# A streaming encoder layer: the indexer's query tiles computed with one moving product of 448 columns for the high and low part of x

## The chip, the cores and the metric

The kernel runs on one core of a Trainium2 chip. The metric is the time of one execution on the device in microseconds (us), the median of several. One further execution is recorded by the profiler, and its trace is what the prediction reads. The engines are called PE (TensorE, matrix products; PEld are its weight loads), ACT (ScalarE), DVE (VectorE), POOL (GpSimd) and SP (SyncE, which here only issues DMAs). PE writes its results to PSUM, eight banks of 512 fp32 columns; ACT and DVE copy them to SBUF.

## The reference

One step of a layer with two branches, for 256 new frames and 32 sampled frames (T = 288 together). Everything starts from one projection of x (288 x 1024) with w_in, whose columns are cut into queries, keys, values and gates of both branches. What matters here is the sparse-attention branch's indexer: eight small query heads qi of 64 each (512 columns of the projection), one indexer key per frame ki and a weight per head wi. They score every key, and each query keeps the best quarter.

```python
p = x @ w_in
(qa, ka, va, oa, za, ia, fa, qb, kb, vb, zb, qi, ki, wi, ga, gb) = jnp.split(p, cuts, axis=-1)
...
sc = jnp.einsum('bqhd,bsd->bqhs', qi, ki).astype(jnp.float32) * (IDX_DIM ** -0.5)
score = jnp.einsum('bqh,bqhs->bqs', wi.astype(jnp.float32) * (IDX_HEADS ** -0.5), jax.nn.relu(sc))
...
_, idx = lax.top_k(score, k_sel)
```

The first 64 frames see only 64 keys and keep all of them, so their indexer queries aren't needed: of qi only the frames 64 to 287 are computed, 224 columns.

## The kernel before

All operands are fp32. To compute an accurate product on PE at the rate of a reduced type, the kernel splits each operand into a high part (a cast to fp32r, by ACT) and a low part (the difference, by DVE), and sums three products: high times high, low x times high weight, high x times low weight.

The work is a list of tiles (`ORDER`), each 128 columns of a weight matrix. Position 0 is the small tile "sm" (indexer key, gates, head weights: 80 columns), positions 1 to 4 are the four indexer query tiles ("qi", two heads each), then qb 0, kb 0, qb 1, kb 1, qb 2 at positions 5 to 9, and so on to the output projection "wo". Weights lie in partitions by k (eight slices of 128), x is transposed: moving operands are `xh[:, k]` and `xl[:, k]`, 288 frames.

The first five tiles (`FIRST = 5`) are computed together while their data arrive: `lead[k]` holds slice k of x and of the five tiles' weights. For k = 0 raw fp32 is used in one product; for k = 1 to 7 `first_products` (L1019 to L1030) runs three groups of five products: high weights with xh, high weights with xl, low weights with xh. Before the data are there, PE runs 15 products of constants (`keep_warm`, L163 to L167). Each of the five tiles has a bank of its own from the ring "side".

From position 5 on the main loop (L1156 to L1170) takes one tile per step t: it issues the loads, splits the weights of later tiles (`split_hi`, L143: ACT casts a whole tile to wh; `split_lo`, L151: DVE makes wl), copies finished tiles out of PSUM (`evac`, L888), and issues the 24 products of tile t (`product`, L974), in the middle of which `side()` issues what is due at this step: scores, gates, attention. Results from tile 5 on go into a ring of two banks ("proj", `out_bank`, L1014), so the products of tile t need the result of tile t - 2 to be copied out.

The order in each engine's queue is the order in which the program emits: the whole body is under a manual schedule. The first five tiles are copied out over the first steps (`held`, L1155): tiles 0 and 1 at step 5, tile 2 at step 6, tile 3 at step 7, tile 4 at step 8. Per step the emitted order is, for t below 8 (`CALM`): `evac(t - 1)`, the held tiles, `split_hi(t + 3)`, `split_lo(t + 2)`; from 8 on: the held tile, `split_lo(t + 2)`, `evac(t - 1)`, `split_hi(t + 3)`. At step 6 `side()` also issues `small_parts` (L275): ACT's copy of the indexer key, DVE's copy into the other half of the partitions, ACT's cast to `kih`, DVE's `kil`, ACT's gate row.

A query tile is copied out by `evac_qi` (L412): ACT casts five pieces from PSUM into the high halves of `qst` and `qis`, then DVE subtracts, writing the low parts into the other half of the partitions, so that one later product covers high and low part of a head.

Late in the program `load_affine` (L1042) reuses the room of xl for z and of xh for the LayerNorm constants.

Of the kernel before, what the change touches and what calls it, by code (L numbers as in the profile page):

```python
# [11 lines left out]
F32R = mybir.dt.float32r  # L12
BF = mybir.dt.bfloat16
AF = mybir.ActivationFunctionType
OP = mybir.AluOpType
# [4 lines left out]
D = 1024  # L20
TP = 256
TS = 32
T = TP + TS
KT = D // 128
# [1 line left out]
BH, BD = 8, 128  # L26
IH, ID = 8, 64
CHUNK = 64
WARM = 15
MID = 4  # L30
FIRST = 5
LATE = 5
# [1 line left out]
SMALL = 80  # L34
LEAD = T + SMALL + 128 * (FIRST - 1)
CALM = 8
PAST = 256
ALPHA = 2.0 ** 0.25
LN_EPS = 1e-5
# [19 lines left out]
def tile_order():  # L59
    order = [("sm", 0)] + [("qi", j) for j in range(4)]  # L60
    for h in range(BH):
        order += [("qb", h), ("kb", h)]
        if h == 3:
            order += [("vb", j) for j in range(8)]
    for h in range(AH):
        for n in ("qa", "ka"):
            order += [(n, 2 * h), (n, 2 * h + 1)]
    order += [("va", j) for j in range(8)]
    order += [("zb", j) for j in range(8)]
    for h in range(AH):  # L70
        for j in (2 * h, 2 * h + 1):
            order += [("oa", j), ("za", j)]
    for j in range(8):
        order += [("gb", j), ("wb", j)]
    for j in range(8):
        order += [("ga", j), ("wa", j)]
    order += [("wo", k) for k in range(KT)]
    return order


ORDER = tile_order()
# [4 lines left out]
def ap_of(t, offset, dims):  # L86
    return bass.AP(tensor=t.tensor, offset=t.offset + offset, ap=dims)
# [3 lines left out]
def body(ctx, tc, a, o):  # L91
    nc = tc.nc
    pe, act, dve, pool, sp = nc.tensor, nc.scalar, nc.vector, nc.gpsimd, nc.sync
# [5 lines left out]
    def sb(name, shape, dt=F32, tag=None, bufs=1):  # L99
        return P.tile(shape, dt, name=name, tag=tag or name, bufs=bufs)  # L100

    def bank(name, n=512):
        return ps.tile([128, 512], F32, name=name, tag="side", bufs=6)
# [19 lines left out]
    store, lazy, masked = {}, {}, []  # L123
# [5 lines left out]
    def load_tile(t):  # L129
        if t >= NT or t in loaded:  # L130
            return
        loaded.add(t)
        stage[t] = sb(f"wst{t}", [128, KT * 128], tag="wst", bufs=8)
        sp.dma_start(stage[t], a["w"][:, t - FIRST])

    def pair(name):
        if name == NT - 1:
            own = sb("wown", [128, 2, KT * 128], F32R, tag="a1")
            return own[:, 0], own[:, 1]
        return (sb(f"wh{name}", [128, KT * 128], F32R, tag="wh", bufs=4),  # L140
                sb(f"wl{name}", [128, KT * 128], F32R, tag="wl", bufs=4))

    def split_hi(t):  # L143
        if t >= NT or t in high:
            return
        load_tile(t)
        split[t] = pair(t)
        act.copy(split[t][0], stage[t])  # L148
        high.add(t)

    def split_lo(t):  # L151
        if t >= NT:
            return
        wh, wl = split[t]
        dve.tensor_tensor(wl, stage[t], wh.bitcast(F32), OP.subtract)  # L155


    xh = sb("xh", [128, KT, T], F32R)
    xl = sb("xl", [128, KT, T], F32R)
    wp = bank("warm_p")  # L160
    ones = nc.const_aps.tensor(1.0, (128, 256), BF)

    def keep_warm(n):  # L163
        for _ in range(n):
            pe.matmul(wp[:, :256], lhsT=ones[:, :128], rhs=ones, start=True, stop=True)  # L165

    keep_warm(WARM)  # L167

    early = sb("early", [128, 2064], tag="v1l")
    bms = early[:, 512:1088].rearrange("p (g t) -> p g t", g=2)  # L170
# [16 lines left out]
    for k in range(KT):  # L187
        raw = lead[k]
# [9 lines left out]
        wh, wl = pair(f"_k{k}")  # L198
# [15 lines left out]
    load_tile(FIRST + 4)  # L214
    sp.dma_start(cki, ap_of(a["cache_idx_k"], 0, [[0, 2], [PAST, 64], [1, PAST]]))

# [74 lines left out]
    def sample_keys():  # L291
        for c, keys in ((slice(0, PAST), cki), (slice(PAST, T), kiT[:, TP:T])):
            act.copy(ksh[:, c], keys)
            dve.tensor_tensor(ksl[:, c], keys, ksh[:, c].bitcast(F32), OP.subtract)
# [113 lines left out]
    kil = sb("kil", [128, TP], F32R, tag="hn", bufs=2)  # L408
    ksh = sb("ksh", [128, PAST + TS], F32R, tag="qph")
    ksl = sb("ksl", [128, PAST + TS], F32R, tag="qpl")  # L410

    def evac_qi(j, p):  # L412
        half = (slice(0, 64), slice(64, 128))
        parts = [(e, slice(t0, t1), slice(c, c + t1 - t0))
                 for e, t0, t1, c in ((0, 64, 128, 128), (0, 128, 256, 0), (1, 64, 256, 192))]
        for e, new, c in parts:
            act.copy(qst[half[e], j, c], p[half[e], new])
        for e in range(2):
            act.copy(qis[half[e], e, j], p[half[e], TP:T])
        for e, new, c in parts:  # L420
            own, other = half[e], half[1 - e]
            dve.tensor_tensor(qst[other, j, c], p[own, new], qst[own, j, c].bitcast(F32), OP.subtract)
        for e in range(2):
            own, other = half[e], half[1 - e]
            dve.tensor_tensor(qis[other, e, j], p[own, TP:T], qis[own, e, j].bitcast(F32), OP.subtract)
# [79 lines left out]
    def load_cache_k():  # L505
        lazy["ckT"] = sb("ckT", [128, 8, PAST], tag="a4")
        sp.dma_start(lazy["ckT"], a["cache_k"])
# [380 lines left out]
    def evac(t, p):  # L888
# [4 lines left out]
        if n == "sm":  # L893
            evac_small(p)
        elif n == "qi":
            evac_qi(j, p)
        elif n == "qb":
            act.copy(qbT[:, j], q)
# [75 lines left out]
    def product(t, side):  # L974
        n, j = ORDER[t]
        if n == "wo":
            natural(t, 0)
            side()
            natural(t, 1)
            return None  # L980
        h, l = moving(n)
        wh, wl = split.pop(t)
        p = out_bank(t)
        for k in range(KT):
            if k == MID:
                side()
            c = slice(128 * k, 128 * k + 128)
            pe.matmul(p[:, :T], lhsT=wh[:, c], rhs=h[:, k], start=(k == 0), stop=False)  # L988
            pe.matmul(p[:, :T], lhsT=wh[:, c], rhs=l[:, k], start=False, stop=False)  # L989
            pe.matmul(p[:, :T], lhsT=wl[:, c], rhs=h[:, k], start=False, stop=(k == KT - 1))  # L990
        return p
# [22 lines left out]
    def out_bank(t):  # L1014
        if t < FIRST:
            return bank(f"pj{t}")
        return ps.tile([128, 512], F32, name=f"pj{t}", tag="proj", bufs=2)

    def first_products():  # L1019
        p = [out_bank(t) for t in range(FIRST)]  # L1020
        for k, (wh, wl) in enumerate(leads):
            raw = lead[0][:, 0:T]
            for w, x in ((wh, raw),) if k == 0 else ((wh, xh[:, k]), (wh, xl[:, k]), ([wl], xh[:, k])):
                for t in range(FIRST):
                    new = slice(CHUNK if ORDER[t][0] == "qi" else 0, T)
                    part = w[0] if t < 2 else w[-1]
                    c0, c1 = (max(0, SMALL + 128 * i) for i in (t - 1, t))
                    pe.matmul(p[t][:c1 - c0, new], lhsT=part[:, c0:c1], rhs=x[:, new],  # L1028
                              start=(k == 0), stop=(k == KT - 1 and w[0] is wl))
        return p  # L1030


# [7 lines left out]
        sp.dma_start(lazy["xs"], ap_of(a["x_nat"], TP * D, [[256, 4], [D, TS], [1, 256]]))  # L1040

    def load_affine():  # L1042
        lazy["z"] = sb("z_", [128, 2, D], tag="xl")
        gb = sb("lngb", [128, 2, D], tag="xh")
        lazy["g"], lazy["b"] = gb[:, 0], gb[:, 1]
        sp.dma_start(gb, ap_of(a["ln_gb"], 0, [[0, 128], [D, 2], [1, D]]))
        for i, n in enumerate("gb"):
            sp.dma_start(lazy[n + "s"], ap_of(a["ln_gb"], D * i, [[256, 4], [0, TS], [1, 256]]))

    at(POS["ga", 3], load_tail)  # L1050
    at(POS["wo", 0], load_affine)

    def statistics(b, r, records):
# [89 lines left out]
    def side():  # L1143
        for fn, args in jobs.pop(cur[0], []):
            fn(*args)
        for g in list(procs):
            if next(g, StopIteration) is StopIteration:
                procs.remove(g)

    first = first_products()  # L1150
    for t in (FIRST, FIRST + 1):
        split_hi(t)
# [3 lines left out]
    for t in range(FIRST, NT - LATE):  # L1156
        cur[0] = t
        for i in range(FIRST, t + 10):
            load_tile(i)
        if FIRST < t < CALM:  # L1160
            evac(t - 1, prev)
        for i in held.get(t, ()):
            evac(i, first[i])
        if t < CALM:
            split_hi(t + 3)
        split_lo(t + 2)
        if t >= CALM:
            evac(t - 1, prev)
            split_hi(t + 3)
        prev = product(t, side)  # L1170
# [84 lines left out]
```

## Time and profile before

| what | us |
|---|---|
| median of 3 runs | 413.38 (413.21 to 413.8) |
| the profiled execution | 413.82 |
| its span, first to last instruction | 412.1 |
| PE busy | 407.7 |
| DVE busy | 316.6 |
| ACT busy | 215.2 |
| POOL busy | 193.0 |

The span leaves out what lies before the first and behind the last instruction. Busy PE time is modelled at its ends, since products are pipelined: how fast they run is read from the distance between their starts. In the rows of the trace the first number is the start in us from the span's start, the second the duration; then come engine, line, operation, tiles written and read, shape and count. A bracket says how long the engine was idle before, and what ended that; where an instruction waited for several things, the one named is the one that came last by the record.

Page of the profile, the costliest groups:

```profile
L989 PE MATMUL pj<-xl,wh 128*128 128x288 f32 x704 | 207.7, 295 | 0.0
L988 PE MATMUL pj<-xh,wh 128*128 128x288 f32 x704 | 207.6, 295 | 0.0
L990 PE MATMUL pj<-xh,wl 128*128 128x288 f32 x704 | 207.5, 295 | 0.0
L155 DVE TENSOR_TENSOR wl<-wst,wh 128x1024 fp32r<-128x1024 f32 x111 | 138.2, 1246 | 22.8 <-ACT wh L148 22.6
L148 ACT CAST wh<-wst 128x1024 fp32r<-128x1024 f32 x111 | 116.3, 1048 | 16.3 <-PE pj L989 5.1
```

Behind the bar stand the busy us, the mean ns of one instruction, and the engine's idle time before the group.

### The profile page before, as it was taken

What the parts mean: (1) busy time and instruction counts of PE and PEld (TensorE: products, weight loads), DVE (VectorE), ACT (ScalarE), POOL (GpSimd) and SP (SyncE); (2) the same over time, 40 slices, a digit from 0 to 9 for tenths busy, and PEclk for the clock granted to TensorE, in tenths of its full rate; (3) what the DMA queues carried; (4) which work ended last, traced back from release to release, by engine and by line L of the source; (5) the groups of instructions that cost most, each with busy time, mean ns of one, the idle gap of its engine ahead of it and who ended that gap; (6) DMA issues with size and microseconds to landing.
All of it is one profiled execution on the core that took longest, in us unless ns stands there. A gap on an engine that the chain in (4) does not pass through costs nothing.

```text
span 412.1 us, 8540 instructions
## 1 busy us (share of the span) xinstructions
PE 407.7 (99%) x3148; PEld 398.0 (97%) x3148; DVE 316.6 (77%) x653; ACT 215.2 (52%) x418; POOL 193.0 (47%) x448
## 2 busy tenths in 40 slices
PE   9999999999999999999999999999999999999996
PEld 7999999999999999999989999999999999999686
DVE  4679879998895878887969877988675566676574
ACT  4787463443765665576645545655434334555202
POOL 0200059993388657769800028547899744000021
PEclk9999999999999999999999999999999999999999
DMA  8987979787955655559944674455656557554014
GB/s 290 389 303 207 310 233 300 271 206 240 386 161 154 226 160 158 166 188 201 286 131 118 167 251 115 144 153 146 171 155 195 163 159 254 175 157 156 2 44 179
DMA packets 43151, 81.09 MB, mean 197 GB/s; under 512 B 20682, under 2 KB 25542, under 8 KB 42182
## 3 DMA queue, kind: packets, MB, share of 16 engines
q1 hardware_dynamic: 42390, 79.73, 62.8%
q10 hardware_dynamic: 720, 0.82, 0.6%
q8 instruction: 24, 0.39, 0.4%
q14 instruction: 17, 0.14, 0.1%
HBM read 73.38 MB, written 9.06 MB: 200 GB/s over the span
## 4 chain that ended last, share of the span: by engine, by line
PE 99%; ACT 0%; ACTq 0%; issue 0%
PE pj L989 27%; PE pj L990 27%; PE pj L988 27%; PE yn L1007 5%; PE pj L1028 4%; PE yn L1011 1%; PE warm_p L165 1%; PE ix L437 0%; PE al L593 0%; PE s L657 0%; PE av L626 0%; PE c L741 0%; PE c L739 0%; PE os L569 0%; PE c L740 0%; PE n L676 0%
## 5 line engine op out<-in xcount | busy, mean ns | idle before, releaser
L989 PE MATMUL pj<-xl,wh 128*128 128x288 f32 x704 | 207.7, 295 | 0.0
L988 PE MATMUL pj<-xh,wh 128*128 128x288 f32 x704 | 207.6, 295 | 0.0
L990 PE MATMUL pj<-xh,wl 128*128 128x288 f32 x704 | 207.5, 295 | 0.0
L155 DVE TENSOR_TENSOR wl<-wst,wh 128x1024 fp32r<-128x1024 f32 x111 | 138.2, 1246 | 22.8 <-ACT wh L148 22.6
L988 PEld LDWEIGHTS pj<-xh,wh 128*128 128x128 f32 x704 | 132.4, 188 | 0.6 <-issue 0.5
L989 PEld LDWEIGHTS pj<-xl,wh 128*128 128x128 f32 x704 | 132.4, 188 | 0.0
L990 PEld LDWEIGHTS pj<-xh,wl 128*128 128x128 f32 x704 | 132.3, 188 | 0.0
L148 ACT CAST wh<-wst 128x1024 fp32r<-128x1024 f32 x111 | 116.3, 1048 | 16.3 <-PE pj L989 5.1
L120 POOL COPY pt<-bm 32x96 f32<-32x96 f32 x128 | 48.8, 381 | 19.9 <-DVE bm L609 10.7
L120 POOL COPY kaT<-kn 32x128 f32<-32x128 f32 x64 | 30.1, 470 | 5.1 <-DVE kn L707 2.5
L120 POOL COPY vn<-qaT 32x128 f32<-32x128 f32 x64 | 29.0, 454 | 2.6
L120 POOL COPY hn<-qaT 32x128 f32<-32x128 f32 x32 | 15.6, 487 | 12.1 <-DVE qaT L683 5.7
L120 POOL COPY hn<-ht 32x128 f32<-32x128 f32 x32 | 14.6, 458 | 9.3 <-DVE ht L683 8.0
L965 POOL COPY mxs<-sg 128x32 f32<-128x32 f32 x8 | 1.7, 211 | 37.0 <-DVE sg L964 36.9
L988 PE MATMUL pj<-bah,wh 128*128 128x288 f32 x64 | 18.9, 296 | 0.0
L989 PE MATMUL pj<-bal,wh 128*128 128x288 f32 x64 | 18.9, 296 | 0.0
L990 PE MATMUL pj<-bah,wl 128*128 128x288 f32 x64 | 18.9, 296 | 0.0
L988 PE MATMUL pj<-bbh,wh 128*128 128x288 f32 x64 | 18.9, 295 | 0.0
L989 PE MATMUL pj<-bbl,wh 128*128 128x288 f32 x64 | 18.9, 295 | 0.0
L990 PE MATMUL pj<-bbh,wl 128*128 128x288 f32 x64 | 18.8, 294 | 0.0
L951 ACT ACTIVATE sg<-pj 128x288 f32<-128x288 f32 x16 | 6.6, 411 | 23.0 <-PE pj L990 23.0
L885 ACT CAST mxh<-sg 128x288 fp32r<-128x288 f32 x8 | 3.5, 433 | 22.1 <-DVE sg L964 22.1
(470 smaller groups left out, 654.1 us busy)
## 6 DMA issues: line engine op xcount, KB each, us to landing
wst<-in_w SPq DMA_DIRECT2D x112, 512.0 KB, 4.4
wst_k<-in_first SPq DMA_DIRECT2D x6, 440.0 KB, 7.9
rscr<-rrow SPq DMA_DIRECT2D x2, 768.0 KB
out_k<-kbT SPq DMA_DIRECT2D x1, 1152.0 KB, 10.2
vrows<-vat SPq DMA_DIRECT2D x8, 144.0 KB, 1.8
stC<-in_state_C SPq DMA_DIRECT2D x1, 1028.0 KB
out_C_sample<-stC SPq DMA_DIRECT2D x1, 1028.0 KB
bm<-rscr SPq DMA_DIRECT2D x1, 1024.0 KB
```

Of the source, the lines that this page charges most:

```text
L120: pool.tensor_copy(out(quads[k], quads[i]), turned(quads[i], quads[k]))
L148: act.copy(split[t][0], stage[t])
L155: dve.tensor_tensor(wl, stage[t], wh.bitcast(F32), OP.subtract)
L165: pe.matmul(wp[:, :256], lhsT=ones[:, :128], rhs=ones, start=True, stop=True)
L885: act.copy(lazy[hi][:, j], v)
L951: act.activation(sg, q, AF.Sigmoid)
L988: pe.matmul(p[:, :T], lhsT=wh[:, c], rhs=h[:, k], start=(k == 0), stop=False)
L989: pe.matmul(p[:, :T], lhsT=wh[:, c], rhs=l[:, k], start=False, stop=False)
L990: pe.matmul(p[:, :T], lhsT=wl[:, c], rhs=h[:, k], start=False, stop=(k == KT - 1))
L1007: pe.matmul(p, lhsT=x[:, k, r], rhs=w[:, c], start=first and i == 0, stop=last and i == 2)
L1011: pe.matmul(p[32 * q:32 * q + 32, 0:256], lhsT=lazy["mxs"][:, k], rhs=stage[t][:, 256 * q:256 * q + 256], start=first, stop=last)
L1028: pe.matmul(p[t][:c1 - c0, new], lhsT=part[:, c0:c1], rhs=x[:, new], start=(k == 0), stop=(k == KT - 1 and w[0] is wl))
```

## The change

For the query tiles and k = 1 to 7, the two products that share the high weights (with xh and with xl, 224 columns each) become one product of 448 columns: xh and xl are now the two halves of one tile `xhl`, and the moving operand reads frames 64 to 287 of both. The results land in two ranges of the tile's bank, columns 0 to 223 and 224 to 447. The products with k = 0 and with the low weights go to the first range as before.

- So that both ranges can be added to from the first product on, each query tile's bank is first written with zeros by a product of a zero weight with 448 columns of ones. These four products stand behind the warm-up, which shrinks from 15 to 8 products. A DVE memset makes the zero weight.
- The order of the products within a k changes: for the high weights tile by tile (both x parts of one tile, then the next tile), then the five with the low weights.
- `evac_qi` first adds the two ranges: ACT copies the second to an SBUF tile, DVE adds the first to it. The five casts and five subtractions then read this SBUF tile instead of the bank.
- At steps 7 and 8 `split_lo(t + 2)` is emitted ahead of the held tile instead of behind it.
- z and the LayerNorm constants share one tile in the room of `xhl`.

```diff
-WARM = 15
+WARM = 8
...
+NEW = T - CHUNK
...
-    xh = sb("xh", [128, KT, T], F32R)
-    xl = sb("xl", [128, KT, T], F32R)
+    xhl = sb("xhl", [128, 2, KT, T], F32R)
+    xh, xl = xhl[:, 0], xhl[:, 1]
...
     keep_warm(WARM)
+    lead_banks = [bank(f"pj{t}") for t in range(FIRST)]
+    zeros = sb("zeros", [128, 128], BF)
+    dve.memset(zeros, 0.0)
+    for t in range(1, FIRST):
+        pe.matmul(lead_banks[t][:, 0:2 * NEW], lhsT=zeros, rhs=nc.const_aps.tensor(1.0, (128, 2 * NEW), BF),
+                  start=True, stop=False)
...
     def evac_qi(j, p):
         half = (slice(0, 64), slice(64, 128))
+        both, p = p, sb(f"qi{j}", [128, T], tag="sg", bufs=3)
+        act.copy(p[:, CHUNK:], both[:, NEW:2 * NEW])
+        dve.tensor_tensor(p[:, CHUNK:], p[:, CHUNK:], both[:, 0:NEW], OP.add)
...
     def first_products():
-        p = [out_bank(t) for t in range(FIRST)]
+        p = lead_banks
         for k, (wh, wl) in enumerate(leads):
             raw = lead[0][:, 0:T]
-            for w, x in ((wh, raw),) if k == 0 else ((wh, xh[:, k]), (wh, xl[:, k]), ([wl], xh[:, k])):
+            for w in (wh,) if k == 0 else (wh, [wl]):
+                low = w[0] is wl
                 for t in range(FIRST):
-                    new = slice(CHUNK if ORDER[t][0] == "qi" else 0, T)
-                    part = w[0] if t < 2 else w[-1]
                     c0, c1 = (max(0, SMALL + 128 * i) for i in (t - 1, t))
-                    pe.matmul(p[t][:c1 - c0, new], lhsT=part[:, c0:c1], rhs=x[:, new],
-                              start=(k == 0), stop=(k == KT - 1 and w[0] is wl))
+                    part = (w[0] if t < 2 else w[-1])[:, c0:c1]
+                    new = slice(T - NEW if ORDER[t][0] == "qi" else 0, T)
+                    n = T - new.start
+                    q = p[t][:c1 - c0, 0:n]
+                    if k == 0:
+                        pe.matmul(q, lhsT=part, rhs=raw[:, new], start=(n == T), stop=False)
+                    elif low:
+                        pe.matmul(q, lhsT=part, rhs=xh[:, k, new], start=False, stop=(k == KT - 1))
+                    elif n == T:
+                        for x in (xh, xl):
+                            pe.matmul(q, lhsT=part, rhs=x[:, k, new], start=False, stop=False)
+                    else:
+                        pe.matmul(p[t][:, 0:2 * n].rearrange("p (a n) -> p a n", a=2), lhsT=part,
+                                  rhs=xhl[:, :, k, new], start=False, stop=False)
...
     def load_affine():
-        lazy["z"] = sb("z_", [128, 2, D], tag="xl")
-        gb = sb("lngb", [128, 2, D], tag="xh")
+        rest = sb("rest", [128, 4, D], tag="xhl")
+        lazy["z"], gb = rest[:, 0:2], rest[:, 2:4]
...
+        ahead = FIRST + 1 < t < FIRST + 4
+        if ahead:
+            split_lo(t + 2)
         for i in held.get(t, ()):
             evac(i, first[i])
         if t < CALM:
             split_hi(t + 3)
-        split_lo(t + 2)
+        if not ahead:
+            split_lo(t + 2)
```

## The prediction

> **What bounds the kernel now.** I read the page's busy times first, then the waits of TensorE (PE), then the order of time on PE, ACT and DVE up to 33 us, the stretch that the change touches.
>
> ```profile
> PE 407.7 (99%) x3148; PEld 398.0 (97%) x3148; DVE 316.6 (77%) x653; ACT 215.2 (52%) x418; POOL 193.0 (47%) x448
> ```
>
> ```profile
> PE warm_p L165 <- PEq L1233: 0.8, 1, 0.8
> ```
>
> PE works 407.7 of 412.1 us, and the only wait on its list is the 0.8 us before its first instruction. So every microsecond that PE is made to wait, or is spared, is a microsecond of the kernel: nothing further on gives it back. The table of PE in order of time (start, duration, engine, line, tiles, count):
>
> ```profile
> 8.63 0.40 PE L1028 MATMUL pj<-xh,whf 128*80 128x288 f32 x2
> ...
> 12.04 0.73 PE L1028 MATMUL pj<-xh,wh_k 128*80 128x288 f32 x5
> ...
> 18.32 0.74 PE L1028 MATMUL pj<-xh,wl_k 128*80 128x288 f32 x5
> 18.89 0.30 PE L988 MATMUL pj<-xh,wh 128*128 128x288 f32 x1
> ...
> 22.07 0.29 PE L988 MATMUL pj<-xh,wh 128*128 128x288 f32 x1
> ...
> 28.41 0.29 PE L988 MATMUL pj<-xh,wh 128*128 128x288 f32 x1
> ...
> 32.28 0.29 PE L988 MATMUL pj<-xh,wh 128*128 128x288 f32 x1
> ```
>
> The first products end at 18.89. Tiles 5, 6, 7 start at 18.89, 22.07 and 22.07 + 3.17 = 25.24; tile 8 at 28.41; tile 9 at 32.28 (tile 8 holds the first scores of the indexer, so it takes 3.87). Beside this PE row run ACT and then DVE:
>
> ```profile
> 18.87 1.05 ACT L148 CAST wh<-wst 128x1024 fp32r<-128x1024 f32 x1 [1.82 <-PE pj L1028]
> 19.82 0.39 ACT L272 COPY early<-pj 80x288 f32<-80x288 f32 x1
> 20.11 0.69 ACT L417 CAST qst<-pj 64x64 fp32r<-64x64 f32 x3
> ...
> 21.21 1.05 ACT L148 CAST wh<-wst 128x1024 fp32r<-128x1024 f32 x1
> 22.29 0.40 ACT L898 COPY qbT<-pj 128x288 f32<-128x288 f32 x1
> 22.59 0.69 ACT L417 CAST qst<-pj 64x64 fp32r<-64x64 f32 x3
> ...
> 26.58 0.41 ACT L279 CAST kih<-early 128x256 fp32r<-128x256 f32 x1 [1.51 <-DVE early L278]
> 27.01 0.54 ACT L286 ACTIVATE gt<-early,cst 4x288 f32<-4x288 f32 x1
> 27.57 0.40 ACT L900 COPY kbT<-pj 128x288 f32<-128x288 f32 x1
> ...
> 28.97 1.05 ACT L148 CAST wh<-wst 128x1024 fp32r<-128x1024 f32 x1
> 30.04 0.69 ACT L417 CAST qst<-pj 64x64 fp32r<-64x64 f32 x3
> ...
> 31.14 0.40 ACT L898 COPY qbT<-pj 128x288 f32<-128x288 f32 x1
> ```
>
> ```profile
> 21.22 0.79 DVE L422 TENSOR_TENSOR qst<-pj,qst 64x64 fp32r<-64x64 f32 x3 [2.91 <-ACT qis L419]
> ...
> 22.45 1.23 DVE L155 TENSOR_TENSOR wl<-wst,wh 128x1024 fp32r<-128x1024 f32 x1
> 23.70 0.79 DVE L422 TENSOR_TENSOR qst<-pj,qst 64x64 fp32r<-64x64 f32 x3
> ...
> 24.93 1.23 DVE L155 TENSOR_TENSOR wl<-wst,wh 128x1024 fp32r<-128x1024 f32 x1
> 26.19 0.30 DVE L278 COPY early<-early 64x288 f32<-64x288 f32 x1
> 27.02 0.43 DVE L280 TENSOR_TENSOR kil<-early,kih 128x256 fp32r<-128x256 f32 x1 [0.53 <-ACT kih L279]
> ```
>
> These rows hold the margin that decides. Tiles from 5 on use two banks in turn, so tile 8 may start only when tile 6 (kb 0) is copied out, and tile 9 when tile 7 (qb 1) is. The copies at 27.57 and 31.14 end at 27.97 and 31.54: tile 8 starts 0.44 us later, tile 9 0.74 us later. And the copy of kb 0 is late not because PE is late (tile 6 ended about 25.4) but because ACT takes its instructions in their order: it stood for 1.51 us before the cast of kih, which waits for DVE's copy at 26.19, which stands behind wl of tile 8 (24.93), which stands behind the subtractions of the second query tile (23.70).
>
> **The change, part by part.**
>
> *Fewer products.* Seven k times four query tiles: 28 times, two products of 224 columns become one of 448. From 12.04 to 18.89 twelve groups of five take 6.85 us, 0.571 each; a 288-column product takes (22.07 - 18.89) / 24 = 0.1325; so one of 224 takes (0.571 - 0.1325) / 4 = 0.1096. No row has 448 columns. The nearest above are these, the first and last of 36 of 512 columns:
>
> ```profile
> 376.55 0.40 PE L1007 MATMUL yn<-wh,mxh 128*128 128x512 f32 x1
> ...
> 384.65 0.40 PE L1007 MATMUL yn<-wh,mxl 128*128 128x512 f32 x1
> ```
>
> 8.10 / 35 = 0.2314. Between 288 and 512 on a line, 448 takes 0.2031 and saves 0.2192 - 0.2031 = 0.016, times 28 = **0.45 us**. Bounds: priced like 512 columns it loses 28 x 0.0122 = 0.34; on the slope from 224 to 288 (0.0229 per 64 columns) it takes 0.190 and saves 0.83. I take 0.45, from the nearest rows on both sides: PE would leave the first products at 18.44. The Trainium skill ("TensorE: Matmul & The Clock Gate", sections "LDWEIGHTS" and "Back-to-back issue gap") puts a 128-column weight load at 128/1.2 = 107 ns, which the measured 110 of a 224-column product agrees with, and a warm product at N/2.4 + 2.5, 189 ns for 448; by it the saving would be an estimated 0.86 us.
>
> *Its operands.* The merged product needs xl at the head of each k. The tightest is k = 2:
>
> ```profile
> 6.42 0.38 DVE L205 TENSOR_TENSOR wl_k<-wst_k,whf 128x208 fp32r<-128x208 f32 x1
> ...
> 7.80 0.46 DVE L194 TENSOR_TENSOR xl<-wst_k,xh 128x288 fp32r<-128x288 f32 x1 [0.20 <-ACT xh L193]
> ```
>
> xl is there at 8.26, PE reaches k = 2 at 8.63: no wait.
>
> *Warm-up and zeros.* Seven warm-ups of 256 columns go, four zero products of 448 come: 15 x 256 = 8 x 256 + 4 x 448 = 3840 columns. At equal time per column this is nothing. The memset for them falls before DVE's first row and is hidden. The parts put in one tile (xhl, rest) move no instruction.
>
> *The evacuation.* Each query tile gets an ACT copy of 128x224, a DVE addition of 128x224, and only then the five ACT casts and five DVE subtractions. Copy: between 0.32 (64x192, one of the casts) and 0.40 (128x288, 22.29), about 0.35. Addition: between 0.38 (128x208) and 0.46 (128x288), 0.39. Hand-overs: 0.03 from ACT to DVE (kih ends 26.99, kil starts 27.02), 0.09 back (26.49 to 26.58). The five casts took 20.11 to 21.21, 1.10; they now read SBUF, where ACT's rows follow each other at 0.34 instead of 0.30 for 288 columns:
>
> ```profile
> 8.81 0.43 ACT L193 CAST xh<-wst_k 128x288 fp32r<-128x288 f32 x1 [0.63 <-DMA wst_k<-in_first]
> 9.15 0.51 ACT L201 CAST wh_k<-wst_k 128x384 fp32r<-128x384 f32 x1
> ```
>
> so 1.30 (bounds 1.10 and, if each pays double that surcharge, 1.50). Start to start, the subtractions take 1.23 and a wl 1.25.
>
> The weight is in what stands behind the waiting instruction. ACT's casts now wait for DVE's addition, and the addition stands in DVE's queue behind the wl emitted before it. Work that ran side by side (casts of one tile beside wl of another) now runs in series.
>
> Chain to tile 8, with ACT's copy of the small tile at 19.82 as before:
> - copy 20.11 to 20.46, addition 20.49 to 20.88, casts from 20.97 to 22.27, subtractions to 23.51, wl 7 to 24.76 (PE wants it at 25.0: just in time);
> - second query tile: its copy is done on ACT meanwhile; addition to 25.15, casts 25.24 to 26.54, subtractions to 27.77, wl 8 to 29.02;
> - DVE's copy, then as before 0.39 to kih, 0.43, 0.56: kb 0 at 30.40, out at **30.80** instead of 27.97.
>
> Tile 8, which could start at 27.96, starts at about 30.85: PE stands 2.9 us.
>
> Chain to tile 9: kil ends 30.28; wl 9, now ahead of the third query tile, to 31.55; addition to 31.94; casts 32.03 to 33.33; subtractions to 34.56 (ACT's wh 10 beside them, 1.07 by 28.97 to 30.04); wl 10 to 35.81; addition to 36.20; casts 36.29 to 37.59; copy of qb 1 out at **37.99**. Tile 8 ends at 30.85 + 3.87 = 34.72; PE stands again, 3.3 us, and tile 9 starts at 38.0 instead of 32.28: **+5.7 us**. After that the queues are regular and tile 10's needs (kb 1 out, wl 10) are met before tile 9 ends.
>
> Moving wl 9 and wl 10 forward covers those two tiles' weights; it puts a further 1.25 us ahead of two additions. The saving of 0.45 is lost in the first stall, unless ACT's start moves with it: the row at 18.87 names PE as what it waited for, and then all shifts by 0.45, +5.2; if it was the weights' landing, +5.7. I take the middle, **+5.4**. The profiled execution took 413.82 (span 412.1 and 1.7 around it), so 419.2; on the median of 413.38 it is **418.8**.
>
> **Rivals.**
>
> *The saving arrives whole, not slower.* If later ACT instructions did not stand behind a waiting cast, kb 0 would be out by the time PE wants it and 0.45 us would remain: 412.9. It decides at one point: kb 0 out before 27.96. Against it speaks the 1.51 us in front of kih, during which tile 6 was finished and its copy ready. With the larger price (0.83) it would be 412.5. Chance 0.12.
>
> *The clock falls in the stall.* At the start PE ran at half speed:
>
> ```profile
> 0.84 3.36 PE L165 MATMUL warm_p<-const-bfloat16-1.0 128*128 128x256 bf16 x15 [0.84 <-PEq L1233]
> ```
>
> ```profile
> 5.33 0.81 PE L1028 MATMUL pj<-wst_k 128*128 128x224 f32 x2
> ```
>
> ```profile
> 5.70 0.63 PE L1028 MATMUL pj<-wst_k 128*128 128x224 f32 x2
> ```
>
> ```profile
> 6.16 0.54 PE L1028 MATMUL pj<-wst_k 128*128 128x224 f32 x2
> ```
>
> ```profile
> 6.35 0.54 PE L1028 MATMUL pj<-wst_k 128*128 128x224 f32 x2
> ```
>
> Equal products lie 0.37 apart at 5.33 and 0.19 at 6.16, after 5 us of work. If standing 3 us brings that back once, half of up to 5 us is lost: +2.5, 421.3. No row of before has a pause that could tell; I give 0.10. The Trainium skill's rule (same page, "Why this matters for your kernels") is no PE gap over about 3 us, else the clock is halved; the two stalls above lie at its edge, and no run here shows it yet.
>
> *Only one stall.* If the copy that frees tile 9's bank, or the SBUF casts, are cheaper than worked out, the first stall (+2.4 at tile 8) stays and most of the second goes: 415.8 to 417. Chance 0.08.
>
> *The merged read waits for all pieces.* If a product over both halves of xhl waited for every xl, k = 1 would wait for the last, near 14.4, and the first products would end some 7 us later, +12 with the stalls: 426. The kernel's tiles are elsewhere followed piece by piece (wl_k by columns). Chance 0.03.
>
> **How the numbers follow.** Forecast 0.67, at 418.8; its bounds: casts at 1.10 take 0.8 off, ACT starting early another 0.5, so 417.5; casts at 1.50 and dearer additions add 1.2: 420.2. Range 416.2 to 420.9, which leaves out the first rival, the upper part of the second and the last. A measurement of this kernel can tell about 0.2%, 0.83 us, from no change. Slower: 0.67 + 0.10 + 0.08 + 0.03 = 0.88. Of the first rival's 0.12 most is within 0.2% (0.09); 0.03 is faster, if the product is at its cheapest.
>
> **What would show it.** Right: a wait of 2 to 3 us on PE before tile 8 and one of about 3 before tile 9, released by ACT's copies (L900, L898 in the numbering of before); casts of a query tile released by DVE's addition; first products some 0.4 us shorter. Wrong: PE still without waits after its first instruction; or an addition that runs before the wl emitted ahead of it; or products of 448 columns above 0.22 us. The second stall hangs on the first three links of its chain; if wl 9 or wl 10 ran elsewhere, it would be shorter by 1.25 each.

## The result, and the profile after

| kernel | median, us | runs | ratio to before |
|---|---|---|---|
| before, same chip | 413.78 | 413.21 to 414.16 (7) | |
| after | 416.02 | 415.70 to 418.38 (7) | 1.0070 (1.0053 to 1.0087) |

The change makes the kernel slower, by 2.2 us in the medians where 5.4 were forecast. Five runs lie between 415.7 and 416.2, two at 418.3. The ratio is one of means, so the two are in it. The forecast range of 416.2 to 420.9 belongs to before's 413.38; from there the ratio gives 416.3, the very lower end of the range. Without the two it would be 1.0054, or 415.6, below the range. One run of all those reported below, a sixth of spread, took 569.04 us at a mean granted clock of 0.657, and is left out of medians and ratios. The profiled execution took 416.18 with a span of 414.5; the one of before had 413.82 and 412.1.

The page's busy line, and then TensorE's whole list of waits (us in total, times, longest):

```profile
PE 407.7 (98%) x3117; PEld 396.4 (96%) x3117; DVE 318.5 (77%) x658; ACT 217.5 (52%) x422; POOL 194.6 (47%) x448
```

```profile
PE pj L998 <- ACT qbT L908: 2.3, 1, 2.3
PE warm_p L166 <- PEq L1258: 0.8, 1, 0.8
```

PE's busy time is what it was, 407.7 us, and one wait is new, for ACT's copy of qb 1, which frees the bank of tile 9. There is none before tile 8. PE in order of time (start, duration, engine, line, tiles, count):

```profile
6.91 0.58 PE L1047 MATMUL pj<-xhl,whf 128*80 128x288 f32 x2
...
12.02 0.42 PE L1047 MATMUL pj<-xhl,wh_k 128*80 128x288 f32 x2
12.28 0.99 PE L1049 MATMUL pj<-xhl,wh_k 128*128 128x448 f32 x4
13.11 0.73 PE L1044 MATMUL pj<-xhl,wl_k 128*80 128x288 f32 x5
...
18.66 0.30 PE L998 MATMUL pj<-xhl,wh 128*128 128x288 f32 x1
...
28.19 0.29 PE L998 MATMUL pj<-xhl,wh 128*128 128x288 f32 x1
...
31.93 0.29 PE L1000 MATMUL pj<-xhl,wl 128*128 128x288 f32 x1
34.54 0.40 PE L998 MATMUL pj<-xhl,wh 128*128 128x288 f32 x1 [2.32 <-ACT qbT L908]
34.78 0.29 PE L999 MATMUL pj<-xhl,wh 128*128 128x288 f32 x1
```

These rows account for the 2.4 us between the two spans. Tile 9 could have started 0.13 behind the product at 31.93, at 32.06; it started at 34.54, 2.48 late, and its first product was followed by the next after 0.24 instead of 0.13: the pause cost **2.59**. From k = 1 on the first products took 18.66 - 6.91 = 11.75, where before took 18.89 - 6.76 = 12.13: **0.38 saved**. They began 0.15 later (6.91 against 6.76; more on that at the end). 2.59 - 0.38 + 0.15 = 2.36.

Why qb 1 is late is read from ACT and DVE, ACT first:

```profile
16.65 1.05 ACT L149 CAST wh<-wst 128x1024 fp32r<-128x1024 f32 x1 [0.27 <-PE pj L1049]
18.42 0.40 ACT L279 COPY early<-pj 80x288 f32<-80x288 f32 x1 [0.72 <-PE pj L1044]
18.72 0.34 ACT L422 COPY qi<-pj 128x224 f32<-128x224 f32 x1
19.52 0.82 ACT L427 CAST qst<-qi 64x64 fp32r<-64x64 f32 x3 [0.46 <-DVE qi L423]
...
20.84 1.05 ACT L149 CAST wh<-wst 128x1024 fp32r<-128x1024 f32 x1
...
27.46 0.40 ACT L910 COPY kbT<-pj 128x288 f32<-128x288 f32 x1
...
32.77 0.81 ACT L427 CAST qst<-qi 64x64 fp32r<-64x64 f32 x3 [1.35 <-DVE qi L423]
...
34.09 0.40 ACT L908 COPY qbT<-pj 128x288 f32<-128x288 f32 x1
```

```profile
19.09 0.39 DVE L423 TENSOR_TENSOR qi<-qi,pj 128x224 f32<-128x224 f32 x1 [1.46 <-ACT qi L422]
19.80 0.93 DVE L432 TENSOR_TENSOR qst<-qi,qst 64x64 fp32r<-64x64 f32 x3 [0.31 <-ACT qst L427]
...
21.19 1.22 DVE L156 TENSOR_TENSOR wl<-wst,wh 128x1024 fp32r<-128x1024 f32 x1
22.72 0.39 DVE L423 TENSOR_TENSOR qi<-qi,pj 128x224 f32<-128x224 f32 x1 [0.31 <-ACT qi L422]
...
31.21 1.23 DVE L156 TENSOR_TENSOR wl<-wst,wh 128x1024 fp32r<-128x1024 f32 x1 [0.77 <-ACT wh L149]
32.35 0.38 DVE L423 TENSOR_TENSOR qi<-qi,pj 128x224 f32<-128x224 f32 x1
```

Read the last rows backwards: qb 1 is copied at 34.09, behind the casts of the fourth query tile, which began at 32.77 once DVE's addition (32.35) was done, which stood behind wl 10 (31.21, the low weights of tile 10). Tile 7 itself had ended by 28.19, the start of tile 8 (24 products of 0.1325 after 18.66, three times). For nearly six microseconds the bank was ready and the copy stood in a queue. The copy of kb 0, at 27.46, was out at 27.86, 0.33 before tile 8 wanted the bank.

### The profile page after: what moved, and what is told of

Read it like the earlier page. It is cut to its first block, busy times and chain, and to the rows that moved or that the text cites. A ratio compares the mean times of both kernels' runs of the same rounds, so it can differ in the third digit from the quotient of the medians.

```text
span 414.5 us, 8484 instructions
## 1 busy us (share of the span) xinstructions
PE 407.7 (98%) x3117; PEld 396.4 (96%) x3117; DVE 318.5 (77%) x658; ACT 217.5 (52%) x422; POOL 194.6 (47%) x448
## 4 chain that ended last, share of the span: by engine, by line
PE 96%; ACT 1%; DMA 1%; DVE 1%; ACTq 0%; issue 0%; SPq 0%
PE pj L999 26%; PE pj L998 26%; PE pj L1000 26%; PE yn L1017 5%; PE pj L1049 1%; DMA rwi<-early 1%; PE pj L1044 1%; PE yn L1021 1%; PE pj L1042 1%; DVE wl L156 1%; PE warm_p L166 0%; PE pj L1047 0%; PE al L603 0%; PE s L667 0%; PE av L636 0%; ACT qst L427 0%
## 5 line engine op out<-in xcount | busy, mean ns | idle before, releaser
L998 PE MATMUL pj<-xhl,wh 128*128 128x288 f32 x704 | 207.7, 295 | 2.3 <-ACT qbT L908 2.3
L999 PE MATMUL pj<-xhl,wh 128*128 128x288 f32 x704 | 207.6, 295 | 0.0
L1000 PE MATMUL pj<-xhl,wl 128*128 128x288 f32 x704 | 207.5, 295 | 0.0
L998 PEld LDWEIGHTS pj<-xhl,wh 128*128 128x128 f32 x704 | 132.4, 188 | 3.2 <-ACT qbT L908 2.6
L999 PEld LDWEIGHTS pj<-xhl,wh 128*128 128x128 f32 x704 | 132.4, 188 | 0.0
L1000 PEld LDWEIGHTS pj<-xhl,wl 128*128 128x128 f32 x704 | 132.2, 188 | 0.0
```

## The experiments

**Theory.** The merging saves its 0.4 us. The evacuation loses more, not by the work it adds but because ACT's queue now waits for DVE and DVE's for ACT, with a copy behind them that frees a bank. The forecast was too high for two reasons that the traces suggest: the subtractions no longer wait for all casts, and ACT entered the chain 1.4 us earlier than assumed (18.42 against 19.82). **Rivals:** the added work itself has to be paid wherever it is put; or the saving is not the merging's.

Spans of single executions differ by when the first products get to full speed, so the table of all traces gives three parts (us): the start of k = 1, from there to the end of the first products, and from there to the end of the span. Where k = 1 begins early, its operands or those of k = 2 can still be on their way: in late_small, qb1_first and longer the second product of k = 2 waited for its xl, which lengthens the second part by 0.3, 0.2 and 0.1, and in before_again (k = 1 at 6.38) the wait of 0.41 came ahead of k = 1. The third part is free of the start.

| kernel | k = 1 | to the end of the first products | rest of the span |
|---|---|---|---|
| before, three traces | 6.76, 6.38, 6.93 | 12.13, 12.03, 12.13 | 393.2, 393.2, 393.1 |
| after, two traces | 6.91, 6.83 | 11.75, 11.75 | 395.8, 395.8 |
| two_products | 6.17 | 12.21 | 397.5 |
| sum_in_bank | 6.44 | 11.76 | 398.4 |
| late_small | 6.08 | 12.09 | 397.6 |
| qb1_first | 6.05 | 11.95 | 394.2 |
| no_ahead | 6.45 | 11.76 | 394.8 |
| longer | 6.62 | 11.86 | 398.1 |
| spread, two traces | 7.22, 6.72 | 11.77, 11.76 | 394.1, 396.2 |
| lean | 7.26 | 11.76 | 393.2 |

### Is the place of one copy the cause?

qb1_first: qb 1 is copied ahead of the fourth query tile, at the head of step 8.

```diff
-        if FIRST < t < CALM:
+        if FIRST < t <= CALM:
             evac(t - 1, prev)
...
-        if t >= CALM:
+        if t > CALM:
             evac(t - 1, prev)
+        if t >= CALM:
             split_hi(t + 3)
```

> The changed kernel with one edit: at step 8 the copy of qb 1 is emitted ahead of the fourth query tile instead of behind it. Queue theory (PE stood 2.32 us before tile 9 because that copy stood in ACT's queue behind casts that wait for DVE's addition, which waits behind wl 10): the wait before tile 9 goes, qb 1 is out about 31.5. The next copy, kb 1, still stands behind the fourth query tile and the first scores: out about 36.1, wanted at 35.2, so PE now waits about 0.9 us before tile 10; time about 414.5. Rival (the low weights made by DVE are what is late): the wait before tile 9 stays above 2 us, time about 416.0.

Measured: 414.38 (413.95 to 414.68, 10 runs), 1.0018 (1.0009 to 1.0027) of before. One row of ACT and one of PE:

```profile
30.41 0.39 ACT L908 COPY qbT<-pj 128x288 f32<-128x288 f32 x1
```

```profile
35.48 0.40 PE L998 MATMUL pj<-xhl,wh 128*128 128x288 f32 x1 [0.75 <-ACT kbT L910]
```

qb 1 is out 3.7 us earlier and tile 9 waits for nothing. The next copy in line, kb 1 (35.02), is now 0.75 late for tile 10. So the place in the queue made the pause, and curing one copy uncovered the next.

### The two splits moved forward

no_ahead: `ahead = False`, so that wl 9 and wl 10 stand behind the query tiles as before; all else as in the change.

> The changed kernel with the moved split_lo put back behind the query tiles at steps 7 and 8. Queue theory: the additions of the third and fourth query tile no longer stand behind wl 9 and wl 10, qb 1 is out about 33.6, PE waits about 1.5 instead of 2.3 us before tile 9, and wl 9 and wl 10 are still in time (31.5 and about 34.4); time about 415.1. Rival (the weights are what is late, as the move suggests): PE waits longer than 2.3 us, or in products with low weights; time above 416.3.

Measured: 414.96 (414.31 to 415.15, 8 runs), 1.0032 (1.0022 to 1.0042).

```profile
33.11 0.40 PE L998 MATMUL pj<-xhl,wh 128*128 128x288 f32 x1 [1.34 <-ACT qbT L908]
```

The pause is 1.0 us shorter, and no product waits for wl 9 or wl 10: this part of the change, which looks like a precaution, makes two fifths of the loss (1.0 of 2.59), because it puts a wl of 1.25 ahead of an addition on which ACT's queue hangs.

### The subtractions

sum_in_bank: the sum is written back to the bank, and casts and subtractions read the bank as before the change. The first lines of the edit (in the others only the source of casts and subtractions changes):

```diff
-        both, p = p, sb(f"qi{j}", [128, T], tag="sg", bufs=3)
-        act.copy(p[:, CHUNK:], both[:, NEW:2 * NEW])
-        dve.tensor_tensor(p[:, CHUNK:], p[:, CHUNK:], both[:, 0:NEW], OP.add)
+        low = sb(f"qi{j}", [128, T], tag="sg", bufs=3)
+        act.copy(low[:, CHUNK:], p[:, NEW:2 * NEW])
+        dve.tensor_tensor(p[:, 0:NEW], low[:, CHUNK:], p[:, 0:NEW], OP.add)
```

> The changed kernel with the sum written back to the query tile's bank; the five casts and five subtractions read the bank, as before the change. Theory A (the subtractions overlap the casts in the changed kernel only because they read SBUF; with the bank as their source they wait for the last cast): DVE's first subtraction starts after the fifth cast, about 1.2 us behind the addition instead of 0.3; kb 0 is out about 29.2, PE waits about 1 us before tile 8 and again before tile 9; time about 417.4. Rival B (the predicted wait before tile 8 failed to come only because ACT began 1.4 us earlier in the profiled run): the subtractions still start about 0.3 us behind the addition, no wait before tile 8, time about 416.0.

Measured: 418.26 (416.95 to 418.51, 4 runs), 1.0105 (1.0088 to 1.0122). DVE, and then PE:

```profile
20.18 0.79 DVE L432 TENSOR_TENSOR qst<-pj,qst 64x64 fp32r<-64x64 f32 x3 [1.15 <-ACT qis L429]
```

```profile
28.51 0.40 PE L998 MATMUL pj<-xhl,wh 128*128 128x288 f32 x1 [0.62 <-ACT kbT L910]
35.10 0.40 PE L998 MATMUL pj<-xhl,wh 128*128 128x288 f32 x1 [2.46 <-ACT qbT L908]
36.05 0.44 PE L998 MATMUL pj<-xhl,wh 128*128 128x288 f32 x1
36.29 0.44 PE L999 MATMUL pj<-xhl,wh 128*128 128x288 f32 x1
```

Reading the bank, the subtractions wait 1.15 for the last cast; reading SBUF (row at 19.80 of after) they wait 0.31 for the first. Tile 9 starts 35.10 - 18.20 = 16.90 us after the first products, 1.02 later than with the change (34.54 - 18.66 = 15.88), though the casts themselves are 0.2 shorter from the bank. A wait before tile 8 is there, of 0.62 where the prediction had 2.9: the overlap accounts for a part of what didn't come, and not for all of it. The last two rows show something else: from 36.05 to 39.3 products are 0.24 apart, twice the usual. It comes back below.

### ACT's start

late_small: the cast wh 7, the last thing on ACT before the small tile, is done three times.

```diff
     split_hi(FIRST + 2)
+    for _ in range(2):
+        act.copy(split[FIRST + 2][0], stage[FIRST + 2])
```

> The changed kernel with the cast wh 7 done three times on ACT instead of once, so that ACT's copy of the small tile begins at about 19.6 us, where the prediction had assumed 19.8, instead of 18.4. Theory (the early start of that copy is worth its full 1.1 to 1.4 us, since everything behind it on ACT and DVE is a chain): kb 0 is out at about 29.0, TensorE waits 0.6 to 0.9 us before tile 8, tile 9 starts 1.0 to 1.3 us later than with the change, counted from the end of the first products, and the time is 417.0 to 417.5 us, or 1.2 more where the clock falls. Rival (there was slack behind the copy): no wait before tile 8 and 416.0 to 416.4 us.

Measured: 418.22 (417.48, 417.55, 418.90, 419.30), 1.0119 (1.0096 to 1.0142). ACT, and then the wait of PE that is new against the change (the one before tile 9 is now 2.5):

```profile
19.99 0.38 ACT L279 COPY early<-pj 80x288 f32<-80x288 f32 x1
```

```profile
PE pj L998 <- ACT kbT L910: 1.3, 1, 1.3
```

Against the end of the first products (18.17 in this trace) the copy begins 1.82 later; in the change it begins 0.24 earlier. These 2.06 us, more than the edit was meant to give, come out as 1.8 us (397.6 against 395.8 for the rest of the span): nearly all of a late start is paid, and the wait before tile 8 appears.

before_again and before_third are the unaltered kernel before.

> The kernel before once more, unaltered, for its trace. Theory (in the profile of before the cast wh 7 waited for a late transfer of its stage, a matter of that one execution): wh 7 begins at 16.6 to 17.0 us as in every trace since, and ACT's copy of the small tile at about 18.6 instead of 19.8. Rival (something in the order of the kernel before holds wh 7 back, and the change took it away): wh 7 begins at 18.9 and the small copy at 19.8 again.

> The kernel before for a third trace. Theory (what holds wh 7 back is something that only the kernel before has): it begins at 18.3 to 18.9 us a third time, and the small copy at 19.3 to 19.9. Rival (chance: two late transfers in a row): 16.6 to 17.6 us, the small copy at about 18.5.

Measured: 413.57 and 413.95. First before_again, then before_third:

```profile
18.39 1.05 ACT L148 CAST wh<-wst 128x1024 fp32r<-128x1024 f32 x1 [1.75 <-PE pj L1028]
19.35 0.38 ACT L272 COPY early<-pj 80x288 f32<-80x288 f32 x1
```

```profile
16.98 1.05 ACT L148 CAST wh<-wst 128x1024 fp32r<-128x1024 f32 x1 [0.66 <-PE pj L1028]
18.82 0.40 ACT L272 COPY early<-pj 80x288 f32<-80x288 f32 x1 [0.79 <-PE pj L1028]
```

The first of the two spoke for something that only the kernel before has, the second against it. wh 7 began at 18.87, 18.39 and 16.98 in three traces of before, at 17.64 in two_products, and at 16.6 to 17.2 in ten traces of the other changed kernels. In the late cases the record of semaphores has the last of the 16 pieces of this weight's transfer 0.1 us before the cast (at 18.77 in before, where the other 15 had landed by 16.8); the row names PE, which had nothing to do with it. So the 19.82 came from a late transfer and not from the order of the instructions, since the third trace, with the same order, has none. Why that piece comes late stays open, and so does whether the kernel before is more prone to it: two of its three traces have it, and in a milder form one of the eleven others.

### Merging alone

two_products keeps everything of the change except the merging.

```diff
-                        pe.matmul(p[t][:, 0:2 * n].rearrange("p (a n) -> p a n", a=2), lhsT=part,
-                                  rhs=xhl[:, :, k, new], start=False, stop=False)
+                        for i, x in enumerate((xh, xl)):
+                            pe.matmul(p[t][:, i * n:i * n + n], lhsT=part, rhs=x[:, k, new], start=False, stop=False)
```

> The evacuation of the change is kept, but each merged product is two again, 224 columns of the high part into one range and 224 of the low part into the other. Theory (the merging alone is what shortens the first products): they end about 0.36 us later than with the change, at 19.0 us, by 28 times the 0.013 us between two products of 224 (0.1096 each) and one of 448 (0.2065), the wait before tile 9 stays 2.0 to 2.3 us, and the time is 416.2 to 416.6 us. Rival (the 0.37 us came from the earlier start of the second round or another part of the change): the first products end at 18.7 us again.

Measured: 417.65, one run. Two rows of PE, 1.72 us apart, which is one k:

```profile
13.48 1.04 PE L1050 MATMUL pj<-xhl,wh_k 128*128 128x224 f32 x8
...
15.20 1.05 PE L1050 MATMUL pj<-xhl,wh_k 128*128 128x224 f32 x8
```

With the merging one k takes 1.66 (6.64 for the four from 12.02 to 18.66 in after): 0.06 less, 0.4 over seven. The saving is the merging's. The clock time that I had expected for their end (19.0) was wrong, 18.38, because k = 1 began at 6.17 instead of 6.91. The time was above the expectation too: after a pause of 2.49 us the products ran at half speed again, 0.24 apart from about 35.6 to 38.9, at a granted clock of 0.50 between 36 and 38.

### Half speed after a pause

longer: ACT copies qb 1's bank twice more ahead of the copy that counts, into columns that kb 1 overwrites later.

```diff
         elif n == "qb":
+            for _ in range(2 if j == 1 else 0):
+                act.copy(kbT[:, j], q)
             act.copy(qbT[:, j], q)
```

> The changed kernel with ACT copying qb 1's bank twice more, into columns that kb 1 overwrites later, before it copies it out: 2 times 0.3 us more before tile 9, so a pause of 2.9 instead of 2.3 us. Theory (a pause of about 2.5 us is the edge from which TensorE's clock is halved for about 3.3 us, which costs 1.3 us): the profile shows products 0.24 us apart some 1.5 us after the pause, and every run takes 417.8 to 419 us. Rival (the lowered clock of the two other kernels has nothing to do with the length of the pause): the products go on 0.13 us apart and the time is 416.5 to 416.9 us.

Measured: 418.07 (417.11, 417.86, 418.27, 418.29), 1.0099 (1.0082 to 1.0116). PE, and then a stretch of 2 us (us, PE busy and products, granted clock, DMA):

```profile
35.09 0.40 PE L1000 MATMUL pj<-xhl,wh 128*128 128x288 f32 x1 [3.06 <-ACT qbT L910]
...
36.67 0.44 PE L1001 MATMUL pj<-xhl,wh 128*128 128x288 f32 x1
```

```profile
36.00:38.00 2.00, 2.00 (x12) 0.58 0.69 258
```

The granted clock of this stretch is 0.58 (0.57 in the next); products are 0.24 apart from 36.4, 1.3 us after PE resumed, to about 39.7. after_again repeats the change itself.

> The changed kernel once more, unaltered. Theory (the pause of 2.3 us before tile 9 lies at the edge from which the clock falls): most runs take 415.7 to 416.2 us, and some about 418.3 with a recorded clock below 1. Rival (the two runs at 418.3 were an accident of that chip): all runs lie within 415.6 to 416.4 us at a recorded clock of 1.

Measured: 416.14 (415.89 to 416.31, 4 runs), none slowed. All runs together, by the longest pause of PE in the profiled execution:

| kernel | pause, us | runs with the lower clock | their times against the others |
|---|---|---|---|
| no_ahead | 1.34 | 0 of 8 | |
| after, after_again | 2.32 | 2 of 11 | 418.3 against 416.0 |
| sum_in_bank | 2.46 | 3 of 4 | 418.3 against 417.0 |
| two_products | 2.49 | 1 of 1 | |
| late_small | 2.50 | 2 of 4 | 419.1 against 417.5 |
| longer | 3.06 | 3 of 4 | 418.1 against 417.1 |

"Lower" is a recorded mean clock of 0.996 or less together with the longer time, or a stretch at half speed in the trace. More runs lose the clock where the pause is longer: 0 of 8 at 1.34, 2 of 11 at 2.32, 9 of 13 from 2.46 on. Length doesn't decide alone: one run of longer kept its clock, and two of the change lost it. The expectation that every run of longer would fall was too strong. That the two slower runs of the change had such a stretch is inferred from their clocks, 0.949 and 0.994: neither left a trace, and a mean of 0.949 is more than a loss of 2.3 us explains.

### The best version

spread was the first try: every step begins with the copy of the tile before, both splits come ahead of the query tile, and the query tiles go to steps 5, 7, 9 and 10. Of its edit, the line that moves the query tiles:

```diff
-    held = {FIRST: (0, 1), FIRST + 1: (2,), FIRST + 2: (3,), FIRST + 3: (4,)}
+    held = {FIRST: (0, 1), FIRST + 2: (2,), FIRST + 4: (3,), FIRST + 5: (4,)}
```

> The changed kernel with another order of the main loop: at every step first the copy of tile t - 1, then both splits, then a query tile; the four query tiles at steps 5, 7, 9 and 10 instead of 5 to 8. Queue theory: every copy and every wl is out over 1 us before PE wants it, PE has no wait after its first instruction, and what is left is the saving of the merged products alone, 0.2 to 0.4 us against before: 413.4 to 413.6. Rival (the merged products or the longer evacuations cost PE something else): no wait, yet 414 or more.

> The kernel with the query tiles at steps 5, 7, 9 and 10 once more, for a second trace of it. Theory (the round trips of the small transfers wn and wp hold DVE up at step 8, by an amount that differs between executions, and with it the query tile of step 9 and what reads it): the time is 414.3 to 416.7 us, and by whatever it exceeds 413.4 there stands a wait of TensorE between 36 and 46 us, for the sample's query rows (qis) or for qb 2 or kb 2. Rival (the scatter comes from another stage): the waits of TensorE before 46 us add up to 0.6 us again, whatever the time.

Measured: 416.20 median for spread (five runs: 414.35, 416.20, 416.28, 416.61 and the profiled one, 414.80), 1.0053 (1.0033 to 1.0074), a miss; spread_again 416.46. DVE in spread, DVE in spread_again, and the two waits of PE behind its first instruction in spread_again:

```profile
32.55 0.17 DVE L316 TENSOR_SCALAR wn<-wn 128x8 f32<-128x8 f32 x1 [1.94 <-DMA wn<-rwi]
33.36 0.17 DVE L316 TENSOR_SCALAR wp<-wp 128x4 f32<-128x4 f32 x1 [0.64 <-DMA wp<-rwi]
```

```profile
32.84 0.17 DVE L316 TENSOR_SCALAR wn<-wn 128x8 f32<-128x8 f32 x1 [2.74 <-DMA wn<-rwi]
35.01 0.17 DVE L316 TENSOR_SCALAR wp<-wp 128x4 f32<-128x4 f32 x1 [2.00 <-DMA wp<-rwi]
```

```profile
PE pj L998 <- ACT qbT L908: 1.3, 1, 1.3
PE ixs L463 <- DVE qis L435: 1.2, 1, 1.2
```

Two small transfers hold DVE up, 2.6 us in one execution and 4.7 in the other, and a query tile now stands behind them: PE waits 0.6 us in the first (for qis) and 2.5 in the second, which with about 0.24 for each restart is what the rest of the span has over before's 393.2 (0.9 and 3.0). In the change's own order these instructions wait for nothing (they come at 34.4, when the data are long there). I had moved work behind a wait that the old order hid.

lean leaves the query tiles at steps 5 to 8, begins every step with the copy of the tile before, puts wl 10 behind the fourth query tile and wh 11 into step 9.

```diff
-        if FIRST < t < CALM:
+        if t > FIRST:
             evac(t - 1, prev)
-        ahead = FIRST + 1 < t < FIRST + 4
+        ahead = FIRST + 1 < t < CALM
...
+        if t > CALM:
+            split_hi(t + 2)
         if not ahead:
             split_lo(t + 2)
-        if t >= CALM:
-            evac(t - 1, prev)
+        if t > CALM:
             split_hi(t + 3)
```

> What is done: the query tiles stay where the change has them (steps 5 to 8), every step begins with the copy of the tile before it, the weight split of tile 10 goes behind the fourth query tile, and those of tile 11 wait for step 9. My theory (the evacuation itself costs nothing that the end shows, only the place of three copies and splits in ACT's and DVE's queues does): kb 0 is out by 27.9 and qb 1 by 31.0 us as in the run that moved qb 1 alone, kb 1 by about 34.2 instead of 35.4, wl 10 is done by about 34.4, TensorE waits for none of the three, the 0.37 us that the merged products save arrives, and the time is 413.1 to 413.4 us on a chip where before takes 413.5 (ratio 0.999 to 1.000). Rival (the longer chain of the evacuation has to be paid somewhere): another tile is late instead, wl 10 or tile 11, a wait of 0.4 us or more stands in the trace, and the time is 413.9 us or more.

Measured: 413.43 (412.67 to 413.96, 11 runs), before on that chip 413.75 (413.34 to 414.33, 15 runs): 0.9990 (0.9981 to 0.9999). ACT, then the whole of PE's list of waits:

```profile
27.82 0.40 ACT L910 COPY kbT<-pj 128x288 f32<-128x288 f32 x1
...
31.44 0.39 ACT L908 COPY qbT<-pj 128x288 f32<-128x288 f32 x1
...
34.50 0.41 ACT L910 COPY kbT<-pj 128x288 f32<-128x288 f32 x1
```

```profile
PE warm_p L166 <- PEq L1259: 0.8, 1, 0.8
```

PE waits for nothing, the rest of the span is before's 393.2, and the 0.3 us of difference is, within the noise, the merging's 0.37. The three copies were out 0.3 to 0.8 later by the clock than expected, since k = 1 began at 7.26, and in time all the same. The same evacuation, with all its added work, costs nothing when each copy stands at the head of its step: kb 0's stood there already, those of qb 1 and kb 1 were moved. The rival that the work must be paid somewhere is out.

## Why the prediction was right and wrong

The direction and the mechanism were right, the size was not: of two forecast pauses one came. That the ratio still touches the range's lower end is luck, since it hangs on the two runs at 418.3.

- **Fewer products** (0.45 forecast): right. The saving was 0.38; a product of 448 columns takes 0.83 / 4 = 0.2065 (rows at 12.28 and 13.11 of after), between the 0.2031 taken and the dearer bound. The Trainium skill's N/2.4 + 2.5 (TensorE: Matmul & The Clock Gate, section "Back-to-back issue gap") gives 189 ns; the measurement decides for 206.
- **Operands, warm-up and zeros** (nothing): right. k = 0 begins at 4.00 in after and 3.99 in before, and no product of after waited. The tightest place was the one named, k = 2: where k = 1 began earlier, it did wait for its xl (0.3 in late_small).
- **Prices of the evacuation**: right in each piece. Copy 0.34 (ACT's row at 18.72; forecast 0.35), addition 0.39 (0.39), casts from SBUF 1.32 from 19.52 to 20.84 (1.30).
- **The mechanism** (additions behind a wl, casts behind additions, a bank-freeing copy behind the casts): right, and shown by qb1_first, no_ahead and lean.
- **The failed step is the chain to tile 8.** It put kb 0 out at 30.80; it was out at 27.86, 2.9 early, so the first pause of 2.9 us did not exist. Two terms of it were wrong, each for about half. "ACT's copy of the small tile at 19.82 as before": it began at 18.42, 1.4 early, since 19.82 contained a late transfer of that execution; late_small shows that a late start is paid almost in full. The prediction had asked what released the row at 18.87, and allowed for a shift of 0.45, but not for a wait that doesn't come back. And "subtractions" after the last cast: they overlap the casts when the source is SBUF, so wl 7 began at 21.19 instead of 22.27 + 1.24 = 23.51, 0.9 more than the early start explains, and wl 8 a further 0.6 (there the addition at 22.72 waited 0.31 for ACT's copy, which the forecast had as done in time). sum_in_bank takes the overlap away, and tile 9 starts 1.0 us later. No run takes away both the overlap and the early start.
- **The chain to tile 9** took what it started with: qb 1 out at 34.49 instead of 37.99, 3.5 early. Of that 2.9 came from the first chain. Of the other 0.6 the overlap left only 0.1, because wl 10 waited 0.77 for wh 10; the rest is that instructions followed each other up to 0.14 closer than priced (wl 9 to the next addition 27.25 to 28.38, 1.13, where 1.27 was taken). The pause that the forecast had as its second, 3.3 us, came as the only one, of 2.48.
- **Rivals.** "Only one stall" had the right time, 415.8 to 417, though it kept the first stall and the second is the one that stayed; 0.08 was too low. "The saving arrives whole" was to be decided by kb 0 being out before 27.96; it was, at 27.86, and the kernel was slower all the same: the test left out that the chain to tile 9 can stall without the first. "The clock falls in the stall" was real, by the recorded clocks in 2 of 11 runs of the change, and for 2.3 us, close to the 2.5 forecast; in the other kernels it cost 1.0 to 1.6. The saving did not arrive whole until lean moved the copies.

## What to carry to other kernels

Before pricing an edit to an evacuation, list what stands behind it in each engine's queue and which of those instructions frees a buffer that the bounding engine wants: here the place of two copies of 0.4 us decided, not the 0.7 us of work added per tile. Put buffer-freeing copies ahead of any work that waits on another engine, and check what the instructions that you move now stand behind. A start time taken from one profile, and a rule that two engines' work is serial, are each worth a second look: look whether the wait named in the row was an accident, and whether the change moves a tile to a memory where the readers no longer wait for each other.

## What the hardware showed unexpectedly

- **A pause of about 2.5 us can halve the granted clock**, with a delay: products go on at full rate for about 1 to 1.3 us, then for 3.3 us they are 0.24 apart instead of 0.13. The Trainium skill (TensorE: Matmul & The Clock Gate, section "Why this matters for your kernels") asks for no gap over about 3 us; here 2.46 us was enough in three of four runs, and 3.06 was not in one of four, so in these runs there is a neighbourhood and no sharp edge.
- **The moment at which PE reaches full speed at the start differs between executions** of kernels whose code up to there is the same: k = 0 began at 4.00 in all eleven traces of the changed kernels, k = 1 between 6.05 (qb1_first) and 7.26 us (lean). The pace is read from the distance between rows: the record of the granted clock has 1.00 throughout this stretch. It shifts everything behind it: the three spans of before (412.1, 411.6, 412.2) follow its k = 1 (6.76, 6.38, 6.93) within 0.1. For runs without a trace this is inferred, but a gain of 0.4 us is better read from stretches between two rows, or from many runs.
- **Subtractions by DVE wait for ACT's last cast when both read one PSUM bank** (1.15 us) and only for the first when both read SBUF (0.31). Whether the chip or the way dependencies are tracked makes the difference, these runs don't tell.
